# The g2 gain moved into the expert rows on GpSimd, additions to x on VectorE, and two raw weight units turned into units for parts

## The chip, the core and the metric

One core of a Trainium2 chip runs the kernel alone. Its engines are TensorE (PE in the profile; PEld is its weight load), VectorE (DVE), ScalarE (ACT), GpSimd (POOL) and SyncE (SP), which issues the DMA transfers of the weights. The metric is the time of one execution on the device in microseconds; a row of the profile gives times from the start of the span.

## The reference, cut to what matters

A conformer-like block (convolution, attention, memory attention, feed-forward) is followed by a second block: four attention mixers, and then a mixture of 16 experts, of which each of the 256 tokens takes two. The change lies in the experts:

```
score = sigmoid(t @ router_w) + router_bias ...      # two experts per token
for e in range(16):
    he = silu(t @ w_gate[e]) * (t @ w_up[e])         # 2048 -> 512
    y = y + combine[:, e:e + 1] * (he @ w_down[e])   # 512 -> 2048
x = x + g2[:, None] * y
return rmsnorm_2(x, final_g)
```

t is 256 x 2048, all in fp32. Each expert has three matrices of 2048 x 512 numbers, 12 MB together, so the experts read 192 loads of 1 MB. g2 is one row of 2048 gains.

## The kernel before

**Tokens and experts.** x, the 256 tokens, lies in two units of 128 x 2048. Each expert gets at most 64 tokens; these are gathered by products with 0/1 matrices (`gather`, L1917), as a high and a low part in fp32r side by side in one 128-column operand. Two experts share a block of 128 slots. After the down projection `give` (L2074, L2075) writes the 64 rows of an expert into half of the pair's unit `E[e]["out"]`: ScalarE copies the low half from PSUM, VectorE adds the high half.

**Scatter.** When the odd expert of a pair has ended, the pair's 128 rows go back to the tokens: for each of the 2 token tiles and 4 column blocks of 512, a product of the combine weights and the rows (`mm`, L2138) into a PSUM bank, on VectorE a product of the bank with g2 into a small tile (`mul`, L2144), and on GpSimd the addition to x (`add`, L2148). `scatter` lists these steps; `pipeline` puts them into the queue "out". The last pair (experts 14 and 15) goes another way, `last`, which the diff doesn't touch.

**Order of the work.** The weights are a list of loads, each with two chunks. `run` works through the chunks in order: before the products of a chunk it issues the splits of later chunks, as far as lookahead and units allow, and after each chunk `step` takes one entry from each background queue. All engines take their instructions in the order in which they were issued so. A split is a copy to fp32r on ScalarE (`wh`, L146) and the rest on VectorE (`wl`, L147), both into one unit for parts; TensorE multiplies by both (L1933, L1934). One chunk of every six isn't split: it stays in its raw unit and is multiplied in fp32 (L1931).

**Units.** There are 19 units of 128 x 2048 numbers. Some of them form the ring: a weight load takes a unit of the ring, and the unit returns to it when the last chunk of the load has been split, or, for an unsplit chunk, multiplied. The others serve parts, rows, x and constants. `resize(n)` moves n units from the free ones to the ring (n < 0: back, as they come free). The ring has 7 units when the experts are set up; `resize(1)` makes that 8, and `resize(-1)` at the down projection of expert 6 makes it 7. At that of expert 8 one unit is taken for the final gain. The rule for the lookahead, with AHEAD = 4, is

```
if c[3] is not None and not c[7] and self.ahead > self.AHEAD - (len(self.free_units) < 3):
    break
```

so that with fewer than three free units one chunk less is split ahead.

Of the kernel before, what the change touches and what calls it, by code (L numbers as in the profile page):

```python
# [45 lines left out]
class Kernel:  # L46
# [1743 lines left out]
    def after_mix(self):  # L1790

        nc, i = self.nc, self.i
# [11 lines left out]
        t = self.small([128, 256], "ln")  # L1804
# [7 lines left out]
        for tt in range(2):  # L1812
            e = slice(tt * 16, tt * 16 + 16)
# [60 lines left out]
        self.most = self.ctile([128, 1], "mosti", mybir.dt.int32)  # L1874
        nc.vector.tensor_copy(self.most, most)
        self.g2 = self.row(self.mod[5:6, :])
        self.resize(1)

    def logits(self, kt):

# [55 lines left out]
    def experts(self):  # L1936
        nc, i = self.nc, self.i
        E = {}

        def after(q, n, f):  # L1940
            for _ in range(n):
                self.bg(q, lambda: None)
            self.bg(q, f)
# [29 lines left out]
        def whole():  # L1973

            return len(self.loads) % 3 == 0

        def spread(n):

            s, ps = slice(n * 512, n * 512 + 512), self.bank()
            nc.tensor.matmul(ps, self.ones[0:1, :], self.fg[0:1, s], start=True, stop=True)  # L1980
            nc.scalar.copy(self.fg[:, s], ps)
            self.done(ps)
# [60 lines left out]
        def down(e):  # L2043
            src = i["exp_w_down_2"][0, e].rearrange("(j p) n -> p j n", p=128)

            def begin():
                st = E[e]
                self.flush("gu", ("hid", e))
                st["o"] = {}
                if e == 15:  # L2050
                    self.AHEAD = 2
                if e == 6:
                    self.resize(-1)
                if e == 8:
                    self.fg = self.U()
                    nc.gpsimd.dma_start(self.fg[0:1, :], i["final_g_2"].rearrange("(a n) -> a n", a=1))
                    for n in range(4):
                        after("fg", 2 if n else 24, lambda n=n: spread(n))
                if e % 2 == 0:
                    st["out"] = self.U()  # L2060

            def mm(j, b, wh, wl, n):
                st = E[e]
                if j == 0:
                    st["o"][b] = self.bank()
                self.both(st["o"][b], st["hl"][:, j * 128:j * 128 + 128], wh, wl, n, j == 0, j == 3)
                if j == 3 and e < 15:
                    self.bg("give", lambda: give(b))

            def give(b):  # L2070

                o = E[e]["o"][b]
                t = E[e - e % 2]["out"][e % 2 * 64:e % 2 * 64 + 64, b * 512:b * 512 + 512]
                nc.scalar.copy(t, o[64:128, :])  # L2074
                nc.vector.tensor_add(t, o[0:64, :], t)  # L2075
                self.done(o)

            def rows(j, c, wh, wl):
                if j == 0 and c == 0:
                    begin()  # L2080
                for n in range(2):
                    mm(j, c * 2 + n, wh, wl, slice(n * 512, n * 512 + 512))
                if j == 3 and c == 1 and e % 2 == 1:
                    after("out", 3, lambda: None)
                    self.pipeline("out", [scatter(e - 1, tt, b) for tt in range(2) for b in range(4)], 1, e < 13)

            def columns(b, c, wh, wl):
                if b == 0 and c == 0:
                    begin()
                for n in range(2):  # L2090
                    mm(c * 2 + n, b, wh, wl, slice(n * 512, n * 512 + 512))
                if c == 1:
                    for f in last(b):
                        self.bg(f"end{b}", f)

            def last(b):

                s = slice(b * 512, b * 512 + 512)
                x = [self.x[tt][:, s] for tt in range(2)]
                ps, t = [None] * 2, [None] * 2  # L2100

                def sums():
                    for tt in range(2):
                        ts = slice(tt * 128, tt * 128 + 128)
                        ps[tt] = self.bank()
                        nc.tensor.matmul(ps[tt], E[e - 1]["ct"][:, ts], E[e - 1]["out"][:, s], start=True, stop=True)
                    for tt in range(2):
                        t[tt] = self.small([128, 512], "ev")
                        nc.vector.tensor_mul(t[tt], ps[tt], self.g2[:, s])
                    self.done(*ps)  # L2110
                    if b == 3:
                        self.free(E[e - 1]["out"])

                def adds():
                    for tt in range(2):
                        (nc.vector if b == 3 or tt else nc.gpsimd).tensor_add(x[tt], x[tt], t[tt])

                def squares():
                    for tt in range(2):
                        j = self.small([128, 512], "pts", 4)  # L2120
                        nc.scalar.activation(j, x[tt], AF.Square, accum_out=self.s2[:, tt * 4 + b:tt * 4 + b + 1])
                return lambda: give(b), lambda: None, sums, adds, squares


            for n in range(4):
                self.add_load(src[:, n:n + 1, :] if e < 15 else src[:, :, n * 512:n * 512 + 512], 2048)
                for c in range(2):
                    self.add_chunk(c * 1024, 1024,
                                   lambda wh, wl, n=n, c=c: (rows if e < 15 else columns)(n, c, wh, wl), c == 1 and whole())

        def scatter(e, tt, b):
            s = slice(b * 512, b * 512 + 512)
            x = self.x[tt][:, s]
            st = {}

            def mm():
                ps = st["ps"] = self.bank()
                nc.tensor.matmul(ps, E[e]["ct"][:, tt * 128:tt * 128 + 128], E[e]["out"][:, s], start=True, stop=True)  # L2138
                if tt == 1 and b == 3:
                    self.free(E[e]["out"])  # L2140

            def mul():
                st["t"] = self.small([128, 512], "ev")
                nc.vector.tensor_mul(st["t"], st["ps"], self.g2[:, s])  # L2144
                self.done(st["ps"])

            def add():
                nc.gpsimd.tensor_add(x, x, st["t"])  # L2148
            return [mm, mul, add]

        def new_block():
            self.XG = self.big.tile([128, 2, 16, 128], F32R, name=self.name("xg"), tag="big")
# [217 lines left out]
```

## Time and profile before

| what | value |
|---|---|
| runs | 2842.44 us median of 3 (2838.5 to 2842.62) |
| profiled execution | 2838.56 us, span 2836.8 us |
| granted TensorE clock, mean | 0.986 |
| busy share of the span | PE 97%, PEld 85%, DVE 74%, ACT 50%, POOL 11% |
| bytes read | 680.66 MB, 241 GB/s over the span |

The span runs from the first to the last instruction. A busy share is a mean over stages with different limits. Matmuls are pipelined and their ends are modelled, so a busy TensorE isn't TensorE at its peak. Durations of GpSimd are rough. An idle stretch of an engine is put down to what ended it. The experts are the last 600 us or so of the span.

### The profile page before, as it was taken

The numbers are of one execution on the slowest core, as the hardware profiler recorded it, in microseconds if no ns is written. First come the engines' busy times: TensorE is split into PE (matmuls) and PEld (weight loads), VectorE is DVE, ScalarE is ACT, GpSimd is POOL, SyncE is SP. The second block draws the span as 40 slices with busy tenths as digits, with TensorE's granted clock in tenths as the row PEclk, the third lists the DMA queues.
The fourth block names the chain that finished last, engine by engine and source line by source line (L and its number), as shares of the span: only waits on it lengthen the run. The fifth ranks groups of instructions, "written<-read, shape, count | busy, mean of one in ns | idle before, by whom it ended". The sixth has DMA issues, their size and how long they took to land. (4 is left out here: it accounts for less than half of the span.)

```text
span 2836.8 us, 43879 instructions
## 1 busy us (share of the span) xinstructions
PE 2737.7 (97%) x17766; PEld 2399.5 (85%) x17766; DVE 2104.4 (74%) x2679; ACT 1416.6 (50%) x2100; POOL 316.0 (11%) x286
## 2 busy tenths in 40 slices
PE   8999999999999999999999998999999899999997
PEld 8898999998998999897989897988886676666664
DVE  5566658899767668877777776656555689998998
ACT  5534444334444545444444454445554476666665
POOL 0000100000100000001000102111001202222223
PEclk9999999999999999999999999999999899999999
DMA  7577654566667765676667673746565599989895
GB/s 256 191 273 257 223 212 159 178 232 216 248 228 268 258 231 219 241 263 216 252 219 262 214 239 122 288 129 216 171 213 180 202 371 343 338 324 343 321 343 210
DMA packets 201427, 685.77 MB, mean 242 GB/s; under 512 B 12148, under 2 KB 15332, under 8 KB 180356
## 3 DMA queue, kind: packets, MB, share of 16 engines
q1 hardware_dynamic: 194336, 662.94, 64.7%
q0 software_dynamic: 5680, 19.53, 2.6%
q8 instruction: 141, 2.31, 0.3%
q10 hardware_dynamic: 1203, 0.45, 0.1%
q14 instruction: 67, 0.54, 0.1%
HBM read 680.66 MB, written 2.20 MB: 241 GB/s over the span
## 5 line engine op out<-in xcount | busy, mean ns | idle before, releaser
L147 DVE TENSOR_TENSOR u<-u,u 128x1024 fp32r<-128x1024 f32 (+3 forms) x1064 | 1255.1, 1214 | 365.9 <-ACT u L146 363.6
L146 ACT CAST u<-u 128x1024 fp32r<-128x1024 f32 (+3 forms) x1064 | 1014.4, 996 | 640.0 <-DMA u<-in_w_in_dram 170.6
L181 PE MATMUL ps<-u,u 128*128 128x256 f32 (+1 forms) x2184 | 625.5, 286 | 2.6 <-ACT u L146 1.7
L183 PE MATMUL ps<-u,u 128*128 128x256 f32 (+1 forms) x2184 | 621.4, 285 | 2.5 <-DVE u L147 2.5
L182 PE MATMUL ps<-u,u 128*128 128x256 f32 (+1 forms) x2184 | 621.2, 284 | 0.5
L181 PE MATMUL ps<-big,u 128*128 128x256 f32 (+1 forms) x1672 | 478.7, 286 | 2.0 <-DVE u L451 0.8
L183 PE MATMUL ps<-big,u 128*128 128x256 f32 (+1 forms) x1672 | 475.0, 284 | 4.3 <-DVE u L147 4.3
L182 PE MATMUL ps<-big,u 128*128 128x256 f32 (+1 forms) x1672 | 474.8, 284 | 0.1
L181 PEld LDWEIGHTS ps<-u,u 128*128 128x128 f32 (+1 forms) x2184 | 421.1, 193 | 9.9 <-ACT u L146 3.8
L183 PEld LDWEIGHTS ps<-u,u 128*128 128x128 f32 (+1 forms) x2184 | 420.9, 193 | 4.5 <-DVE u L147 4.3
L182 PEld LDWEIGHTS ps<-u,u 128*128 128x128 f32 (+1 forms) x2184 | 421.2, 193 | 1.7 <-DVE u L1309 1.3
L181 PEld LDWEIGHTS ps<-big,u 128*128 128x128 f32 (+1 forms) x1672 | 321.3, 192 | 11.0 <-issue 4.6
L183 PEld LDWEIGHTS ps<-big,u 128*128 128x128 f32 (+1 forms) x1672 | 321.3, 192 | 5.9 <-DVE u L147 5.7
L182 PEld LDWEIGHTS ps<-big,u 128*128 128x128 f32 (+1 forms) x1672 | 321.4, 192 | 1.1 <-DVE big L1309 0.6
L171 PE MATMUL ps<-u,u 128*128 128x512 f32 x736 | 292.0, 397 | 5.4 <-ACT u L146 5.3
L172 PE MATMUL ps<-u,u 128*128 128x512 f32 x736 | 289.4, 393 | 8.0 <-DVE u L147 7.6
L173 PE MATMUL ps<-u,u 128*128 128x512 f32 x736 | 288.1, 391 | 0.0
L1171 DVE SCALAR_TENSOR_TENSOR u<-u,cols,u 128x2048 f32<-128x2048 f32 x96 | 226.3, 2357 | 5.6 <-DMA u<-in_ada_w_dram 5.6
L1933 PE MATMUL ps<-u,xg 128*128 128x512 f32 x416 | 187.8, 451 | 0.4 <-DVE xg L1924 0.3
L172 PEld LDWEIGHTS ps<-u,u 128*128 128x128 f32 x736 | 139.0, 189 | 39.8 <-DVE u L147 12.5
L171 PEld LDWEIGHTS ps<-u,u 128*128 128x128 f32 x736 | 138.9, 189 | 39.6 <-ACT u L146 8.7
L1934 PE MATMUL ps<-u,xg 128*128 128x512 f32 x416 | 167.6, 403 | 0.8 <-DVE u L147 0.7
(374 smaller groups left out, 3077.9 us busy)
## 6 DMA issues: line engine op xcount, KB each, us to landing
u<-in_w_in_dram SPq DMA_DIRECT2D x128, 1024.0 KB, 5.1
u<-in_ada_w_dram SPq DMA_DIRECT2D x96, 1024.0 KB, 5.3
u<-in_w_up_dram SPq DMA_DIRECT2D x88, 1024.0 KB, 5.5
u<-in_exp_w_gate_dram SPq DMA_DIRECT2D x64, 1024.0 KB, 9.6
u<-in_exp_w_up_dram SPq DMA_DIRECT2D x64, 1024.0 KB, 7.3
u<-in_exp_w_down_dram SPq DMA_DIRECT2D x64, 1024.0 KB, 8.2
u<-in_w_down_dram SPq DMA_DIRECT2D x44, 1024.0 KB, 6.6
u<-in_w_o_dram SPq DMA_DIRECT2D x16, 1024.0 KB, 7.1
```

Of the source, the lines that this page charges most:

```text
L146: self.nc.scalar.copy(wh[:, :width], wt)
L147: self.nc.vector.tensor_sub(wl[:, :width], wt, wh[:, :width].bitcast(F32))
L171: nc.tensor.matmul(o, xh[:, ts], wh[:, cs], start=first, stop=False)
L172: nc.tensor.matmul(o, xh[:, ts], wl[:, cs], start=False, stop=False)
L173: nc.tensor.matmul(o, xl[:, ts], wh[:, cs], start=False, stop=last)
L181: nc.tensor.matmul(o, wh[:, cs], xh, start=first and m % 2 == 0, stop=False, **kw)
L182: nc.tensor.matmul(o, wh[:, cs], xl, start=False, stop=False, **kw)
L183: nc.tensor.matmul(o, wl[:, cs], xh, start=False, stop=last, **kw)
L1171: nc.vector.scalar_tensor_tensor(a, wt, self.col["c"][:, kt:kt + 1], a, op0=OP.mult, op1=OP.add)
L1933: self.nc.tensor.matmul(ps, x, wh[:, s], start=start, stop=False)
L1934: self.nc.tensor.matmul(ps, x, wl[:, s], start=False, stop=stop)
```

## The change

The gain g2 is no longer multiplied into each scattered product. GpSimd multiplies it into the pair's 128 rows, in place, one column block at a time, once for both token tiles (`scale`); after two empty steps TensorE scatters the rows, and one step later VectorE adds the bank to x. The pieces go by column block first, then token tile. An empty item between two pieces takes the place of the empty step that `pipeline` put after each step; for expert 13 there is neither, before and after.

The ring gives two of its 7 units to the free ones instead of taking one, the step at expert 6 goes, and AHEAD is 5 instead of 4 from the set-up of the experts on (2 from expert 15, as before).

```
         self.g2 = self.row(self.mod[5:6, :])
-        self.resize(1)
+        self.resize(-2)
+        self.AHEAD = 5
...
                 if e == 15:
                     self.AHEAD = 2
-                if e == 6:
-                    self.resize(-1)
...
-                    self.pipeline("out", [scatter(e - 1, tt, b) for tt in range(2) for b in range(4)], 1, e < 13)
+                    self.pipeline("out", [it for b in range(4) for tt in range(2)
+                                          for it in ([scatter(e - 1, tt, b), []] if e < 13 else [scatter(e - 1, tt, b)])], 1)
...
+            def scale():
+
+                o = E[e]["out"][:, s]
+                if tt == 0:
+                    nc.gpsimd.tensor_mul(o, o, self.g2[:, s])
...
-            def mul():
-                st["t"] = self.small([128, 512], "ev")
-                nc.vector.tensor_mul(st["t"], st["ps"], self.g2[:, s])
+            def add():
+                nc.vector.tensor_add(x, x, st["ps"])
                 self.done(st["ps"])
-
-            def add():
-                nc.gpsimd.tensor_add(x, x, st["t"])
-            return [mm, mul, add]
+            return [scale, lambda: None, lambda: None, mm, add]
```

## Rows read from the trace of the kernel before

**Rows 1.** The page's engine table: busy us (share of the span) xinstructions.

```profile
PE 2737.7 (97%) x17766; PEld 2399.5 (85%) x17766; DVE 2104.4 (74%) x2679; ACT 1416.6 (50%) x2100; POOL 316.0 (11%) x286
```

**Rows 2.** Busy us by stretch, seven bursts; last three columns: clock, DMA share, GB/s.

```profile
2404.00:2432.00 28.00, 25.98 (x113) 18.09 (x112) 27.23 (x26) 14.21 (x19) 15.58 (x8) 0.94 0.96 366
2478.00:2510.00 32.00, 29.78 (x134) 21.41 (x134) 30.48 (x31) 15.56 (x21) 20.74 (x12) 0.95 0.88 324
...
sum 191.00, PE 175.35 PEld 123.64 DVE 186.62 ACT 98.05 POOL 118.74; mean PE 25.05 PEld 17.66 DVE 26.66 ACT 14.01 POOL 16.96
```

**Rows 3.** The same view, the six stretches between the bursts.

```profile
sum 274.00, PE 273.83 PEld 189.66 DVE 239.00 ACT 217.00 POOL 18.18; mean PE 45.64 PEld 31.61 DVE 39.83 ACT 36.17 POOL 3.03
```

**Rows 4.** Timeline of a burst: start, us, engine, line, [idle before, released by].

```profile
2493.42 3.42 DVE L147 TENSOR_TENSOR u<-u,u 128x1024 fp32r<-128x1024 f32 x2
2496.76 0.68 DVE L2144 TENSOR_TENSOR ev<-ps,u 128x512 f32<-128x512 f32 x1
...
2493.57 2.18 POOL L2148 TENSOR_TENSOR u<-u,ev 128x512 f32<-128x512 f32 x1 [1.76 <-DVE ev L2144]
...
2497.59 0.47 PE L1933 MATMUL ps<-u,pts 128*128 128x512 f32 x1 [2.02 <-DVE ev L2144]
```

**Rows 5.** Instructions of one line: count, ns min/median/max, first and last start.

```profile
L147 DVE TENSOR_TENSOR u<-u,u x265: 1206/1216/2316, 2298.8 to 2779.5; 128x1024 fp32r<-128x1024 f32 x133
...
L2148 POOL TENSOR_TENSOR u<-u,ev x50: 1259/2190/2266, 2332.5 to 2777.9; 128x512 f32<-128x512 f32 x50
...
L2075 DVE TENSOR_TENSOR u<-ps,u x52: 674/683/685, 2320.6 to 2771.9; 64x512 f32<-64x512 f32 x52
...
L2281 POOL TENSOR_TENSOR u<-u,u x1: 1736/1736/1736, 2827.6 to 2827.6; 128x512 f32<-128x512 f32 x1
```

**Rows 6.** The same view, weight loads issued by SyncE, 2300 to 2780 us.

```profile
L128 SPq DMA_DIRECT2D u<-in_exp_w_down_dram x53: 327/341/2986, 2301.2 to 2775.4; - x53
L128 SPq DMA_DIRECT2D u<-in_exp_w_gate_dram x52: 367/378/528, 2304.6 to 2757.3; - x52
L128 SPq DMA_DIRECT2D u<-in_exp_w_up_dram x52: 367/368/2301, 2312.5 to 2764.8; - x52
```

**Rows 7.** Who waited for whom, 2300 to 2780: us in total, times, longest.

```profile
SPq L128 <- DVE u L147: 307.6, 86, 8.3
...
PEld ps L1934 <- DVE u L147: 17.5, 49, 0.6
...
PE ps L1933 <- DVE ev L2144: 11.5, 6, 2.0
...
ACT u L146 <- PE ps L1934: 55.6, 49, 3.2
...
ACT u L146 <- DMA u<-in_exp_w_down_dram: 2.0, 2, 1.5
```

**Rows 8.** Busy us by stretch, columns as in rows 2.

```profile
2390.00:2400.00 10.00, 10.00 (x40) 6.74 (x39) 9.23 (x14) 7.82 (x11) 0.00 (x0) 1.00 1.05 386
...
2210.00:2220.00 10.00, 3.50 (x17) 3.53 (x17) 7.70 (x26) 1.04 (x1) 4.38 (x4) 0.50 0.29 106
```

**Rows 9.** Two loads: issue and landing (line view), first product (timeline).

```profile
L128 SPq DMA_DIRECT2D u<-in_exp_w_gate_dram x1: 378/378/378, 2380.1 to 2380.1; - x1
...
DMA to landing us min/median/max: 7.5/7.5/7.5
...
2396.31 0.39 PE L1933 MATMUL ps<-u,xg 128*128 128x512 f32 x1
...
L128 SPq DMA_DIRECT2D u<-in_exp_w_gate_dram x1: 499/499/499, 2752.0 to 2752.0; - x1
...
DMA to landing us min/median/max: 10.4/10.4/10.4
...
2767.74 0.39 PE L1933 MATMUL ps<-u,xg 128*128 128x512 f32 x1
```

## Prediction

> **What bounds the kernel now.** I read the page's engine table first [rows 1]: TensorE is busy 97% of the span, every other compute engine well below (VectorE 74%). A busy TensorE need not be a full one, so I cut the expert stage, where all edits lie, into stretches. After each odd expert up to 13 there is a burst in which the rows of a pair of experts are scattered into x: seven bursts in all. In the seven stretches that hold them TensorE is busy 175.35 of 191 us [rows 2]; in the six stretches between them 273.83 of 274 us [rows 3]. So what another engine can still give back in this stage lies nearly all in the bursts: 15.65 us of idle TensorE. Two burst stretches also ran at a mean clock of 0.94 and 0.95 [rows 2], which costs 28 x 0.06 + 32 x 0.05 = 3.3 us more. Together **19.0 us**, 2.7 per burst.
>
> Who holds TensorE up there? VectorE is busy 186.62 of the 191 us of the bursts [rows 2]. The timeline of one burst shows how [rows 4]: while GpSimd adds a 128x512 piece to x (2.18 us), two weight splits (L147) take 3.42 us together, and the scaling product (L2144) of an earlier scatter comes only after them, at 2496.76. TensorE waits 2.02 us for just that, since the bank which it wants next is the one that L2144 reads. The view of one line gives 1206/1216/2316 ns for a split [rows 5]: alone it costs 1.21 us, beside a GpSimd addition up to 1.1 us more. GpSimd's addition itself ranges from 1.26 to 2.27 us, median 2.19 [rows 5]: each lengthens the other.
>
> Behind VectorE stands the weight stream. All 53 + 52 + 52 = 157 loads of the stage's middle are issued from 2301.2 to 2775.4 us [rows 6], one per 474.2/157 = 3.02 us, and SyncE's wait before them is mostly for L147 (307.6 us), for a unit to come free [rows 7]. The loads are a full 1 MB: at 386 GB/s, the rate with the DMA engines fully busy [rows 8], one needs 2.72 us. DMA isn't the bound on average, but has only a tenth to spare, and it lives on the number of raw units ahead. ScalarE's copies already waited for a load, 2.0 us in two pieces [rows 7]: the present ring is just deep enough.
>
> **The change, part by part.** *GpSimd.* Per burst, eight additions L2148 go and four multiplications of the same shape come. No such multiplication is in this stage's trace; the nearest is the one of the last step, 1.74 us [rows 5], inside the additions' range, so I price it as an addition. Each overlaps one split, so VectorE gets back 4 x 1.1 = 4.4 us per burst; the bounds are 0 (a multiplication that blocks twice as long) and 8.8.
>
> *VectorE.* Eight products from PSUM (0.68 us [rows 4]) become eight additions that read one operand from PSUM and write x. The row with that very form, a sum of PSUM and a unit (L2075), takes 0.68 us too [rows 5]. Nothing gained or lost in busy time; bounds are zero both ways, as neither end of the two rows differs. But the read of the bank is queued one chunk after the scatter instead of two (the step spacing of two chunks stays), so one split fewer stands before the bank comes free: 1.2 to 2.3 us earlier.
>
> *TensorE* scatters the same 8 products, three chunks later. They now wait for GpSimd. The scaling of a column block is issued four chunks or more after the rows are complete and three chunks before its product; a chunk is half a load, 1.51 us, so 4.5 us stand against at most 2.27 us. I cost it at nothing; what covers it are those three chunks, and without cover it costs up to 2.27 us for each of 28 blocks. The row unit is freed three chunks later; that falls within the next pair's first chunks, and both row units fit in the count below.
>
> Sum for the bursts: 4.4 us plus an earlier bank against 2.7 us that TensorE loses. I take 16.0 of the 19.0 us; the lower bound is 8, if the unchanged 8 x 0.68 us of evacuations keep half of the lag.
>
> *The units.* There are 19. x takes 2, h2 2, g2 1. Before: a raw ring of 8 (7 from expert 6), so 6 (7) for parts and rows; with fewer than three free, the split stops with 4 chunks ahead. After: a ring of 5 from the start of the experts, 9 left: 6 chunks ahead, and 5 from expert 8, where the final gain takes a unit. So a load may start three raw units later, but two chunks earlier: 3 x 3.02 - 2 x 1.51 = 6.0 us late up to expert 6; then 2 x 3.02 - 2 x 1.51 = 3.0; from expert 8 2 x 3.02 - 1.51 = 4.5.
>
> What does that meet? Two gate loads, each at the tightest place of its pair, one early and one late in the stage [rows 9]. The one issued at 2380.1 lands 7.5 us later, at 2387.6, and TensorE uses it at 2396.31: 8.7 us after landing (the product is found by counting chunks in order). The one of 2752.0 lands at 2762.4 and is used at 2767.74: 5.3 us. ScalarE's copy and VectorE's split need some 2.3 us of that (an estimate: a split's 1.22 and no more than that for the copy). So 8.7 - 6.0 - 2.3 = +0.4 early, 5.3 - 4.5 - 2.3 = -1.5 us late: about even in the first pairs, and the more so in the one or two that are only 3.0 late, but short by one to two in the last three. A shortage counts once per pair, since in a burst the stream gets ahead again. ScalarE and VectorE take their work in order, so a copy that waits for its load holds up the evacuations behind it; these have TensorE's 5 or 6 split chunks as cover. I take **+6 us** for the stage, bounds 0 and 27 (seven pairs with 6.0 us late on a cover of 5.3, and half a load each).
>
> *Five chunks ahead.* ScalarE waits 55.6 us for TensorE to free a unit for parts, and weight loads wait 17.5 us in 49 pieces for L147 [rows 7]. One chunk more lets splits run ahead over the evacuations. Much of that waiting lies under products still running (the stretches between bursts show 0.17 us idle), so of 0 to 17.5 us I take 2.5, near zero.
>
> Start: while the routing is worked out the ring is full and the DMA engines are busy 0.29 of the time [rows 8]; three units fewer in that queue leave five loads, some 15 us of work, in hand, so I cost the start at nothing. Nothing is added to the last expert's path: 0.
>
> Sum: -16.0 + 6.0 - 2.5 = **-12.5 us**. The profiled execution took 2838.56 us; 2838.56 - 12.5 = 2826.1. The median of the runs is 3.9 us above it, 2842.44, and would give 2829.9. I say **2828 us**.
>
> **A rule of the skill.** The row says that a GpSimd operation costs a split 1.1 us, half of its own 2.19 us [rows 5]. The Trainium skill, "SBUF — State Buffer", section "SBUF: two separate sides", says that a VectorE operation with two SBUF inputs and a GpSimd operation that reads SBUF exclude each other for a whole instruction. By that and the profile's own span, four operations fewer would be worth 4 x 2.19 = 8.8 us per burst instead of 4.4; by either, more than TensorE loses there, so the sum stays. The same rule speaks against the change where GpSimd is the one that waits: the fourth rival.
>
> **Rivals.** *The ring gives it back.* For it: 10% spare on DMA, copies that already waited. If every pair is short by half a load (1.4 us) plus the delay of the evacuations behind it (about 1), the ring costs 7 x 2.4 = 17 us against 18.5: about 2841, no change.
>
> *Half a cure.* VectorE stays near full in a burst because the count of its instructions is the same; the bursts give 8, the ring takes 6: about 2840.
>
> *The ring becomes the bound, slower.* Place: the gate and up loads before each burst. If the lookahead buys nothing (splits stall on the late load, so ring 5 means three loads later and no chunks back), loads come 9.1 us late up to expert 6, 6.0 after; against covers of 8.7 and 5.3 less 2.3 us the pairs lose 2.7 and 3.0, and with the evacuations (about 1.5) some 4.2 each, 29 us: -18.5 + 29, about 2852. It decides once a pair loses more than 18.5/7 = 2.6 us.
>
> *TensorE waits for GpSimd.* VectorE is 98% busy in bursts, GpSimd has to get in between. If each of 28 scalings makes the scatter wait 1 us, 28 us are lost: about 2855. Against it: the additions never exceeded 2.27 us with VectorE that full [rows 5].
>
> **How the numbers follow.** Forecast (bursts cured, ring at 10 us or less): 0.58, 2812 to 2836. No change (first two rivals): 0.24. Ring as bound: 0.14. GpSimd wait: 0.04. 0.2% of 2842.44, 5.7 us, is what a measurement here can tell; the forecast's upper edge and the first rival's lower edge both touch 2836.7, so faster 0.60, same 0.23, slower 0.17. Leaving out 0.1 above and 0.1 below: **2811 to 2847**.
>
> **What would show it.** Right: 28 multiplications and no L2148; splits over 2 us halve in number; TensorE's wait for the bank (11.5 us [rows 7]) gone and burst stretches above 97% busy. ScalarE's waits for DMA grow from 2 us to some tens, without TensorE's idle time growing between bursts. Wrong: TensorE idle before products on weights while the load is on its way, above all in the second half of a pair, or a wait of the scatter for the new multiplication.

## The result and the profile after

The changed kernel takes 2869.23 us (median of 6 runs) beside 2841.31 us for the kernel before on the same chip: ratio 1.0097, 95% interval 1.0082 to 1.0112, 27.5 us slower. The forecast was 2828 us, in a range of 2811 to 2847. The profiled execution took 2869.81 us, its span 2868.0 us, 31.2 us above the span before; the mean granted clock fell from 0.986 to 0.981.

The engine table of the page, which answers to [rows 1]:

```profile
PE 2748.4 (96%) x17766; PEld 2408.2 (84%) x17766; DVE 2094.6 (73%) x2679; ACT 1420.8 (50%) x2100; POOL 289.7 (10%) x258
```

VectorE and GpSimd both have less to do than before, and the kernel is slower. The view by line and form, 2300 to 2780 us (count | busy us, mean ns | idle before, released by), shows the splits and GpSimd's two kinds of work, first of the kernel before:

```profile
L147 DVE TENSOR_TENSOR u<-u,u 128x1024 fp32r<-128x1024 f32 x265 | 349.6, 1360 | 21.1 <-ACT u L146 20.4
L2148 POOL TENSOR_TENSOR u<-u,ev 128x512 f32<-128x512 f32 x50 | 104.9, 2107 | 418.1 <-DVE ev L2144 418.1
L2007 POOL TENSOR_SCALAR bias<-cst,pos,comb 128x64 f32<-128x64 f32 x24 | 19.3, 817 | 0.0
```

and of the kernel after:

```profile
L147 DVE TENSOR_TENSOR u<-u,u 128x1024 fp32r<-128x1024 f32 x248 | 304.2, 1254 | 51.6 <-ACT u L146 49.5
L2140 POOL TENSOR_TENSOR u<-u,u 128x512 f32<-128x512 f32 x24 | 55.2, 2311 | 388.8 <-DVE u L2074 388.8
L2008 POOL TENSOR_SCALAR bias<-cst,pos,comb 128x64 f32<-128x64 f32 x24 | 44.1, 1850 | 0.0
```

A split became 106 ns shorter on average: 106 x 265 = 28 us in some six bursts (50 of the 56 additions lie in these 480 us), 4.5 us per burst, as much as the prediction gave VectorE back. But the splits aren't all of VectorE's work. Two other operations became longer (same two views, before and then after):

```profile
L2038 DVE TENSOR_TENSOR pts<-bias,pts 128x256 fp32r<-128x256 f32 x13 | 5.4, 417 | 0.0
L1904 DVE TENSOR_TENSOR o<-pos,cst 128x128 f32<-128x128 f32 x12 | 2.9, 284 | 0.0
```

```profile
L2039 DVE TENSOR_TENSOR pts<-bias,pts 128x256 fp32r<-128x256 f32 x13 | 12.0, 924 | 0.0
L1905 DVE TENSOR_TENSOR o<-pos,cst 128x128 f32<-128x128 f32 x12 | 9.5, 829 | 0.0
```

Such operations stand at the start of a burst, where the multiplications now fall. By the engine tables VectorE's busy time shrank by only 2104.4 - 2094.6 = 9.8 us, 1.4 us per burst. So some of the relief stayed, and still the kernel lost time. The stretches show why. Each burst begins with the gate and up stage of an odd expert. I cut the first 25 us of these seven stages out of each trace, from the first product of the stage (columns as in [rows 2], whose burst stretches begin some ten us later). The kernel before:

```profile
2394.00:2419.00 25.00, 25.00 (x90) 15.74 (x89) 24.42 (x24) 18.03 (x21) 8.77 (x4) 1.00 1.04 401
...
sum 175.00, PE 174.35 PEld 110.33 DVE 170.10 ACT 123.63 POOL 67.97; mean PE 24.91 PEld 15.76 DVE 24.30 ACT 17.66 POOL 9.71
```

The kernel after, same stages:

```profile
2327.00:2352.00 25.00, 19.77 (x61) 11.26 (x60) 22.43 (x23) 16.05 (x20) 16.06 (x8) 0.93 0.85 316
2404.00:2429.00 25.00, 19.68 (x62) 11.55 (x61) 21.99 (x22) 16.45 (x20) 15.31 (x7) 0.93 0.87 313
...
sum 175.00, PE 144.02 PEld 86.24 DVE 163.94 ACT 114.96 POOL 100.97; mean PE 20.57 PEld 12.32 DVE 23.42 ACT 16.42 POOL 14.42
```

Before, TensorE was idle for 175 - 174.35 = 0.65 us of these 175 us; after, for 31.0 us. On top of it the granted clock, 1.00 in all seven before, averages 0.92 after (0.93, 0.93, 0.86, 0.93, 1.00, 0.86, 0.93), which costs some 0.08 x 175 = 14 us (an estimate). So about 45 us are lost in a place that lost nothing. The six stretches that lie between these seven, before and then after:

```profile
sum 295.00, PE 279.83 PEld 205.81 DVE 259.94 ACT 197.44 POOL 67.45; mean PE 46.64 PEld 34.30 DVE 43.32 ACT 32.91 POOL 11.24
```

```profile
sum 318.00, PE 312.13 PEld 229.67 DVE 256.69 ACT 208.53 POOL 7.86; mean PE 52.02 PEld 38.28 DVE 42.78 ACT 34.75 POOL 1.31
```

There the idle time of TensorE fell from 295 - 279.83 = 15.2 us to 318 - 312.13 = 5.9, and the clock, 0.97 in two of the six before, is 1.00 in all of them: some 12 of the 19 us that the prediction counted did come back. GpSimd is busy 14.4 us of each of the seven stretches instead of 9.7, with half the scatter operations: the multiplications run at the front, and the small products for the next pair's combine weights (L2008) followed them. The DMA engines moved 309 to 333 GB/s there; before, 388 to 401 in six of the seven and 346 in one.

The waits after, 2300 to 2780 us (in total, times, longest), which answer to [rows 7]:

```profile
ACT u L146 <- DMA u<-in_exp_w_down_dram: 52.6, 43, 3.9
...
PEld ps L1935 <- DVE u L147: 45.4, 40, 2.7
...
PE ps L1935 <- DVE u L147: 27.3, 24, 2.3
...
ACT u L146 <- DMA u<-in_exp_w_up_dram: 26.9, 21, 4.9
...
ACT u L146 <- DMA u<-in_exp_w_gate_dram: 16.8, 16, 1.7
...
PE ps L1934 <- DVE u L2149: 0.5, 1, 0.5
```

The wait for the bank is gone (11.5 us before, 0.5 now). ScalarE waits 96.3 us for loads instead of 2.0, and TensorE waits 27.3 us for a split. The waits for a split show at the start of one burst. VectorE and GpSimd there (timeline, as in [rows 4]):

```profile
2332.95 0.68 DVE L2074 TENSOR_TENSOR u<-ps,u 64x512 f32<-64x512 f32 x1
2333.67 1.23 DVE L147 TENSOR_TENSOR u<-u,u 128x1024 fp32r<-128x1024 f32 x1
2334.81 1.52 DVE L2039 TENSOR_TENSOR pts<-bias,pts 128x256 fp32r<-128x256 f32 x1
2336.36 0.68 DVE L2074 TENSOR_TENSOR u<-ps,u 64x512 f32<-64x512 f32 x1
2337.07 1.23 DVE L147 TENSOR_TENSOR u<-u,u 128x1024 fp32r<-128x1024 f32 x1
...
2333.72 2.33 POOL L2140 TENSOR_TENSOR u<-u,u 128x512 f32<-128x512 f32 x1 [90.91 <-DVE u L2074]
2337.12 2.32 POOL L2140 TENSOR_TENSOR u<-u,u 128x512 f32<-128x512 f32 x1 [1.07 <-DVE u L2074]
2340.58 2.34 POOL L2140 TENSOR_TENSOR u<-u,u 128x512 f32<-128x512 f32 x1 [1.14 <-DVE u L2074]
```

and TensorE (same view, same kernel):

```profile
2334.95 0.50 PE L1935 MATMUL ps<-u,xg 128*128 128x512 f32 x1 [1.54 <-DVE u L147]
...
2338.35 0.80 PE L1935 MATMUL ps<-u,xg 128*128 128x512 f32 x1 [2.21 <-DVE u L147]
```

The first two multiplications start 0.1 us after the end of a give (L2074: 2332.95 + 0.68 = 2333.63, then 2337.04). In program order each stands steps later, but GpSimd has nothing else to do and goes as soon as its rows are written. Beside the first one a 128x256 subtraction (L2039), 0.42 us without GpSimd (timeline of the run with the multiplications on VectorE and the same ring), takes 1.52 us; the give and the split behind it come that much later, and TensorE, which has no split chunk in hand, waits 2.21 us for that split. Not all of this is GpSimd's doing. In the run with a marker (below, same ring), where GpSimd multiplies only from 2341.91 on, TensorE waits before the same two products:

```profile
2333.01 0.50 PE L1937 MATMUL ps<-u,xg 128*128 128x512 f32 x1 [1.56 <-DVE u L147]
2335.32 0.49 PE L1937 MATMUL ps<-u,xg 128*128 128x512 f32 x1 [1.11 <-DVE u L147]
```

The first wait is there without GpSimd; of the second, 2.21 - 1.11 = 1.1 us are GpSimd's, as much as the subtraction became longer.

### The profile page after: what moved, and what is told of

It is laid out like the page before. It is cut to its first block, busy times and chain, and to the rows that moved or that the text cites. A ratio compares the mean times of both kernels' runs of the same rounds, so it can differ in the third digit from the quotient of the medians.

```text
span 2868.0 us, 43868 instructions
## 1 busy us (share of the span) xinstructions
PE 2748.4 (96%) x17766; PEld 2408.2 (84%) x17766; DVE 2094.6 (73%) x2679; ACT 1420.8 (50%) x2100; POOL 289.7 (10%) x258
## 5 line engine op out<-in xcount | busy, mean ns | idle before, releaser
L147 DVE TENSOR_TENSOR u<-u,u 128x1024 fp32r<-128x1024 f32 (+3 forms) x1064 | 1228.8, 1186 | 394.6 <-ACT u L146 390.5
```

The lines of the kernel that those rows point to most:

```text
L147: self.nc.vector.tensor_sub(wl[:, :width], wt, wh[:, :width].bitcast(F32))
```

## The experiments

Two theories stood at first. **Theory R**: the smaller ring costs all of the loss, and the scatter part is a gain. **Theory S**: GpSimd's multiplications fall on the gives at the burst's start and hold up the splits. Differences in us below are differences of ratios times 2840 us; an interval of 0.0015 either way is 4 us.

**Halves of the change.** The scatter part alone, with the ring of before (8, then 7 raw units) and four chunks ahead:

```diff
-        self.resize(-2)
-        self.AHEAD = 5
+        self.resize(1)
...
+                if e == 6:
+                    self.resize(-1)
```

> The scatter part alone: g2 into the rows on GpSimd and the addition on VectorE as in the changed kernel; ring (8, then 7) and lookahead (4) as before. Theory R (the smaller ring costs all of the loss, and the scatter part is a gain): faster than before, 2822 to 2833 us; ScalarE's waits for loads stay at some 2 to 10 us between 2300 and 2780. Theory S (GpSimd's multiplications fall on the gives at the start of a burst and hold up the splits there): as slow as the changed kernel or half of it, 2855 to 2870 us, with TensorE waiting for L147 some 25 us.

2852.92 us, ratio 1.0047 [1.0029, 1.0064]: 13 us slower, just under the range of theory S. Theory R falls. The units part alone is the kernel before with the two lines of the units and without `resize(-1)`; the ring alone is the same without `AHEAD = 5`:

> The units part alone: ring 5 from the start of the experts and AHEAD 5; scatter as before (product with g2 on VectorE, addition on GpSimd). Theory R: slower than before by at least the whole loss, 2865 to 2885 us, since the old burst still lengthens eight splits instead of four. Theory S: 2836 to 2848 us, no change.

2874.41 us, 1.0134 [1.0117, 1.0151].

> The ring of 5 with AHEAD 4, scatter as before: three, then two raw units fewer, and the units that come free serve only one more split chunk. Theory R: slower than e2 by the chunk that no longer runs ahead (1.5 us earlier issue per load and less cover): 2870 to 2895 us. Theory S: within 5 us of before.

2871.98 us, 1.0113 [1.0091, 1.0135]: 32 us slower, and five ahead gives nothing back (0.0021 between the two, within their intervals). So neither theory holds alone: both halves are losses.

**Without the multiplication.** From the kernel after, and then from the scatter part alone:

```diff
-                if tt == 0:
-                    nc.gpsimd.tensor_mul(o, o, self.g2[:, s])
+                pass
```

> The changed kernel without GpSimd's multiplication by g2 (the gain is left out of the rows); all else as changed. Theory R: the late loads stay, so it gains only the lengthened splits: 28 x 1.1 us at most where TensorE stands right behind them, 2850 to 2868 us. Theory S: the loss goes, 2830 to 2842 us.

2843.5 us, 1.0013 [1.0004, 1.0023].

> The scatter part alone with the ring of before, as in the run of the scatter part alone (2852.9 us), but GpSimd's multiplication by g2 is left out (so the experts' gain is missing from the result; the rest is computed). Theory S (what GpSimd multiplies at a burst's start costs all of that run's 13 us, and the scatter's other steps are a gain): 2820 to 2832 us. Rival (the scatter's new order costs by itself: the additions to x on VectorE, or the products three chunks later): 2845 to 2856 us.

2828.23 us, 0.9955 [0.9939, 0.9971]. These four runs make a square:

| | GpSimd multiplies | multiplication left out | difference |
|---|---|---|---|
| ring 8/7, four ahead | 1.0047 | 0.9955 | 26 us |
| ring 5, five ahead (after) | 1.0097 | 1.0013 | 24 us |
| difference | 14 us | 16 us | |

Within the intervals the two costs add. The 27.5 us are 26 for the multiplications, 14 for the units, and a gain of 13 from the rest of the scatter's new form (the additions taken off GpSimd, which the next runs price at 21 us, less 8). In the 25 us stretches, the scatter part alone and then the same without the multiplication:

```profile
sum 175.00, PE 154.58 PEld 97.73 DVE 169.85 ACT 115.11 POOL 97.59; mean PE 22.08 PEld 13.96 DVE 24.26 ACT 16.44 POOL 13.94
```

```profile
sum 175.00, PE 166.05 PEld 107.39 DVE 163.94 ACT 122.09 POOL 3.56; mean PE 23.72 PEld 15.34 DVE 23.42 ACT 17.44 POOL 0.51
```

11.5 us of idle TensorE come with the multiplications, and a clock of 0.86 to 1.00 (mean 0.93) instead of 1.00 in all seven, an estimated 0.07 x 175 = 12 us: together 24 of the 26.

**What the old additions cost.** The kernel before without its GpSimd additions (that line replaced by `pass`), with its own ring and with a ring of 5:

> The kernel before without GpSimd's additions to x in the scatter (the experts' rows don't reach x; the rest is computed). It prices the 56 additions. By the prediction (each lengthens a split by 1.1 us, and 19 us of TensorE's idle time and clock go with them): 2820 to 2826 us. Rival (they lie beside slack, and TensorE's waits for a bank come of the products' own lag on VectorE): 2832 to 2840 us.

2817.51 us, 0.9925 [0.9899, 0.9951]: 56 additions cost 21 us, 0.38 us each. 28 multiplications cost 26 us, 0.93 us each.

> Ring of 5, four chunks ahead, the scatter of before, without GpSimd's additions to x (left out as in the run beside it). With the additions that ring cost 32 us. If the smaller ring is dear only where GpSimd makes the splits long (a unit is held longer, so its next load starts later): 2826 to 2842 us, that is some 15 us or less above the run beside it. Rival (the ring is too short for the loads by itself): 2850 to 2862 us, some 30 us above it.

2840.34 us, 1.0002 [0.9991, 1.0014]: the ring of 5 still costs 22 us when GpSimd adds nothing, against 32 beside the additions. It is too short without them too.

**Place.** The multiplications of the scatter part alone, written to one small tile, so that each waits for TensorE's products of the block before:

```diff
-                    nc.gpsimd.tensor_mul(o, o, self.g2[:, s])
+                    E[e]["sg"] = self.small([128, 512], "ev")
+                    self.small([128, 512], "ev")
+                    nc.gpsimd.tensor_mul(E[e]["sg"], o, self.g2[:, s])
...
-                nc.tensor.matmul(ps, E[e]["ct"][:, tt * 128:tt * 128 + 128], E[e]["out"][:, s], start=True, stop=True)
+                nc.tensor.matmul(ps, E[e]["ct"][:, tt * 128:tt * 128 + 128], E[e]["sg"], start=True, stop=True)
...
-            return [scale, lambda: None, lambda: None, mm, add]
+            return [lambda: None, lambda: None, scale, mm, add]
```

> The scatter part alone with the ring of before; the four GpSimd multiplications per burst stay, but each writes one small tile, so that the second to fourth wait until TensorE's products of the block before have read it: they are spread over the burst, some four chunks (6 us) apart, instead of following the gives at its start (1, 2 and 3 each within some 3.5 us). Theory S as to the place (25 us are lost because the multiplications fall together at the burst's start, on the gives and on splits that are just in time): 2829 to 2841 us. Rival (a GpSimd multiplication costs VectorE the same wherever it falls in the burst): 2849 to 2857 us, as the run of the scatter part alone.

2841.07 us, 1.0005 [0.9991, 1.0019], at the upper edge of theory S's range. GpSimd's timeline in it:

```profile
2399.49 1.31 POOL L2143 TENSOR_TENSOR ev<-u,u 128x512 f32<-128x512 f32 x1 [45.96 <-DVE u L2075]
2403.08 2.28 POOL L2143 TENSOR_TENSOR ev<-u,u 128x512 f32<-128x512 f32 x1 [2.27 <-DVE u L2075]
2415.21 2.07 POOL L2143 TENSOR_TENSOR ev<-u,u 128x512 f32<-128x512 f32 x1 [9.86 <-PE ps L2147]
2421.42 1.58 POOL L2143 TENSOR_TENSOR ev<-u,u 128x512 f32<-128x512 f32 x1 [4.14 <-issue]
```

The same work on the same engine, of which only the last two of four come later, costs 14 us instead of 26: 0.50 us each. In the 25 us stretches of its trace TensorE is busy 156.46 us, little more than the 154.58 without pacing, but at a mean clock of 0.97 instead of 0.93 (the profiled execution, 2847.24 us, was one of the longer ones). That the place counts, and not only how much longer VectorE's work becomes, is seen in the engine tables of the five kernels:

| GpSimd's work in the scatter | VectorE busy with it, without it | longer by | time lost by it |
|---|---|---|---|
| 56 additions, kernel before | 2104.4, 2063.7 us | 40.7 us | 21 us |
| 28 multiplications, scatter part alone | 2086.3, 2064.5 us | 21.8 us | 26 us |
| 28 multiplications, paced | 2090.2, 2064.5 us | 25.7 us | 14 us |

One operation lengthens VectorE's work by 0.73 us (additions), 0.78 or 0.92. A microsecond of that costs the kernel 0.5 us, 1.2 us and again 0.5 us. Holding the small products for the combine weights back as well (their tile taken from the same small one) changes nothing:

> The paced run with the ring of before (2841.1 us), and in addition GpSimd's four small products for the next pair's combine weights (L2007) write the same small tile, so that they start only when the burst's last product has read it, and not right behind the last multiplication, in the burst. Theory: part of the 13 us that pacing did not give back is theirs, since they now fall into the burst (3.2 us long after the burst before, 7.9 us in the run of the scatter part alone): 2828 to 2837 us. Rival (the 13 us are the four multiplications' own, wherever they fall): 2838 to 2844 us.

2842.39 us, 1.0015 [1.0, 1.003]. So the 14 us aren't theirs, and are put down to the multiplications. In the changed kernel, with its ring of 5, the same pacing gives nothing:

> The kernel after itself (ring of 5, five ahead) with the multiplications spread over the burst through one small tile, as in the paced run with the ring of before. If place and ring are costs of their own that add: 2869 less the 12 us that pacing gave there, 2853 to 2861 us. If pacing gives more where every load is just in time: 2843 to 2852 us. If it gives nothing here (the ring alone holds the stage): 2866 to 2872 us.

2868.72 us, 1.0104 [1.0074, 1.0134]. It may be that there the first two multiplications, which pacing leaves where they were, are enough; why the last two cost nothing in it is not settled.

A first try at place failed by its own construction: GpSimd was to wait until VectorE had come to its step (`vector.memset(mk)`, then a `gpsimd.tensor_mul` on `mk` ahead of the multiplication).

> The kernel after, but each GpSimd multiplication waits until VectorE has come to its step of the scatter (VectorE writes a 128x8 marker there, GpSimd reads it first), so that it no longer starts right behind the give. Theory S as to the place (the multiplication costs because it falls on the gives and splits at the burst's start): 2846 to 2860 us. Rival (a GpSimd operation costs VectorE the same wherever it falls): 2866 to 2876 us; rival of the prediction (TensorE then waits for GpSimd): above 2876 us, with waits of the scatter product for the multiplication.

2896.54 us, 1.0201 [1.0172, 1.0229], and TensorE's waits in it, 2300 to 2780 us, are led by

```profile
PE ps L2148 <- POOL u L2144: 42.1, 6, 7.9
```

In program order the gives and the splits of chunks up to five ahead stand before the marker, and VectorE came to it only behind them (at 2340.69 in the burst above), while the product that needs the multiplication comes three chunks later. So TensorE waited for VectorE's place in its queue, 7.9 us at the longest. The run says nothing of place.

**The other engine.** One word (`gpsimd` to `vector` in the multiplication), with the ring of before:

> The scatter part alone with the ring of before, the four multiplications by g2 per burst on VectorE instead of GpSimd, at the same steps. Per burst 4 x about 0.7 us more for VectorE, no GpSimd operation. Theory S (overlap with GpSimd is the cost): 2825 to 2840 us, and splits over 2 us gone from the bursts. Rival (VectorE is full in a burst, so any work for it costs its whole length, 7 x 2.8 = 20 us, and GpSimd's cost less): 2850 to 2865 us.

2834.89 us, 0.9990 [0.9977, 1.0003]: 16 us better than on GpSimd, 10 us above no multiplication at all. Part of these 10 us is a wait of the scatter's products for the multiplication (2300 to 2780 us):

```profile
PE ps L2145 <- DVE u L2141: 5.4, 7, 0.9
```

In the 25 us stretches TensorE is busy 160.60 us, and 166.05 without the multiplication: the same 5.4 us. With the scatter two chunks apart in the last burst too, and then with each burst's scatter three chunks later (`after("out", 6, ...)` for 3):

> A try for the fastest kernel: the ring of before, multiplications on VectorE, and the scatter's steps two chunks apart after the last odd expert too (there they are one apart, and that burst was 2.6 us longer than the other six). 2830 to 2835 us; if the last burst's length has another cause: 2834 to 2838 us.

2838.73 us, 0.9997 [0.9983, 1.0011]: the padding gains nothing.

> The same, with every burst's scatter starting three chunks later, clear of the gives and of the gather's last steps. As VectorE takes its work in order, these multiplications do move. If VectorE's load at the start of a burst is what costs: 2825 to 2831 us. Rival (the count of VectorE's operations costs, not their place): within 3 us of the run beside it.

2828.7 us, 0.9963 [0.9951, 0.9976]. The same instructions three chunks later are worth 10 us, and this version beats both kernels, by 10 us and by 38. The wait of the products for the multiplication is gone from its trace, so at least that part of the 10 us is a wait and not VectorE's load at the burst's start; no run separates the rest. Its 25 us stretches:

```profile
sum 175.00, PE 166.03 PEld 106.86 DVE 169.81 ACT 125.04 POOL 4.53; mean PE 23.72 PEld 15.27 DVE 24.26 ACT 17.86 POOL 0.65
```

TensorE is busy 166.03 us, as in the run without the multiplication (166.05), and the clock is 1.00 in all seven. VectorE did 28 multiplications more, at 0.68 us each; placed there they cost nothing that this view shows. The one word in the kernel after:

> The kernel after with one word changed: the multiplications by g2 on VectorE instead of GpSimd, at the same steps (ring of 5, five ahead). With the ring of before that word was worth 18 us (2852.9 to 2834.9). If GpSimd's overlap is the cost here too: 2846 to 2853 us. Rival (with every load just in time the stream sets the pace and VectorE's longer queue counts in full): 2858 to 2870 us.

2874.76 us, 1.0125 [1.0106, 1.0144], with the same trap as the marker:

```profile
PE ps L2144 <- DVE u L2140: 24.0, 6, 5.1
```

Where VectorE is not as far ahead as the program has it, its place in the program is a late place. Less these 24 us it would be where the first range of its expectation had it, but that is only argued.

**Ring sizes.**

> The kernel after with 6 raw units instead of 5 (one unit less for parts, still five ahead). If what the ring costs falls off steeply with each unit: 2853 to 2860 us. If each unit costs a like share of the 16 us between the scatter part alone and the kernel after: 2860 to 2866 us. If five chunks ahead, not the ring, is what costs: 2867 to 2872 us.

2849.11 us, 1.0039 [1.0025, 1.0053]: faster than any line of the expectation. The sixth unit, with one unit less for parts, is worth 16 us, and with it the kernel is no slower than the scatter part alone on the ring of before (1.0047). The loss lies between five and six units.

> As the run with the multiplications on VectorE, but with a ring of 7 raw units up to expert 6 and 6 after, and five chunks ahead: the five chunks ahead at the price of one raw unit instead of two or three. If a unit less is hidden while no GpSimd operation holds up the splits: 2820 to 2838 us, below the run with the ring of before. Rival (each raw unit taken costs a third of what three cost, 32 us): 2838 to 2855 us.

2842.14 us, 1.0014 [1.0001, 1.0028], against 0.9990 with the ring of before: 7 us dearer. But this can't be put down to the ring. TensorE's waits in it, 2300 to 2780 us, are led by

```profile
PE ps L2146 <- DVE u L2142: 18.2, 7, 2.8
```

where the run with the ring of before had 5.4: with five chunks ahead more splits stand before the multiplication in VectorE's queue, the trap of the marker again. What the unit itself costs, this run doesn't show.

> The fastest kernel so far (multiplications on VectorE, scatter three chunks later, two chunks apart; 2828.7 us with the ring of before) with a ring of 6 throughout and five chunks ahead. If a ring of 6 is deep enough once a burst no longer holds up VectorE: 2820 to 2827 us, by the 0.7 to 0.9 us that each even gate and up stage gains with more units for parts. Rival (a raw unit less costs more than that): 2830 to 2842 us.

2829.88 us, 0.9961 [0.9947, 0.9975]: the same as with the ring of before (0.9963). Where the burst no longer holds VectorE up, a ring of 6 with five ahead costs and gains nothing that these runs can tell.

## Why the prediction was wrong, step by step

**What bounds the kernel** held as a reading, and misled as a measure. The 15.65 us of idle TensorE and the low clock are where the GpSimd additions were: without them the kernel is 21 us faster, near the 19.0. But I read "VectorE full" as one condition of a whole burst. The first 25 us of the stage in which it lies were full on VectorE (24.3 of 25 us) and on TensorE alike, with no idle time to give back and none to spare. That stretch I never priced, because nothing was lost in it.

**The step that failed** is the first: "Each overlaps one split, so VectorE gets back 4 x 1.1 = 4.4 us per burst", turned into a gain of 16.0 us. The scatter part alone came out as 13 us lost. The 4.4 us met the 4.5 by which the splits became shorter, but as VectorE's gain it was too much, and that the two agree is luck: not every multiplication falls on a split, and one operation lengthens VectorE's work by some 0.75 us, not 1.1. VectorE got back 18.1 us in the scatter part alone, 2.6 per burst, and 1.4 per burst in the kernel after. What decided was the place, which the step left out: the four multiplications follow at once behind the gives, where no split chunk is in hand, and there a microsecond of VectorE's time cost 1.2 us, where one beside the old additions had cost 0.5. I had taken the multiplication's place from the program ("issued four chunks or more after the rows are complete"). On GpSimd, idle here, that order set nothing; the row that showed it was the release of L2148 by L2144 in [rows 4], a GpSimd operation that started as soon as its data was there.

**GpSimd as something to wait for** at nothing: right. No wait of the scatter product for L2140 is among TensorE's waits after. The fourth rival did not happen; the runs where the product did wait (42.1, 24.0, 18.2 and 5.4 us) had put VectorE's place in its queue before it.

**The earlier bank** was right: 11.5 us of that wait became 0.5.

**The ring** was mis-sized: +6 us for it, measured 14 and 16 us in the square for ring and lookahead together, for which I had 6.0 - 2.5 = 3.5. (The upper bound of 27 doesn't come out of the terms given for it: 7 x (6.0 + 2.3 - 5.3) is 21, with half a load each 31.) The lateness itself was nearly right. The load that answers to the first of [rows 9] (second gate load of expert 5; line view, then the timeline of ScalarE and TensorE, after):

```profile
L128 SPq DMA_DIRECT2D u<-in_exp_w_gate_dram x1: 379/379/379, 2396.4 to 2396.4; - x1
...
DMA to landing us min/median/max: 8.3/8.3/8.3
...
2404.88 1.05 ACT L146 CAST u<-u 128x1024 fp32r<-128x1024 f32 x1 [1.61 <-DMA u<-in_exp_w_gate_dram]
...
2406.32 0.39 PE L1934 MATMUL ps<-u,xg 128*128 128x512 f32 x1
```

It lands at 2396.4 + 8.3 = 2404.7 and is used 1.6 us later, where 8.7 us stood before: 7.1 us late, where I had 6.0. What failed is "A shortage counts once per pair, since in a burst the stream gets ahead again". In six of the seven 25 us stretches of the kernel before the DMA engines are fully busy (share 1.02 to 1.04, about 400 GB/s): that is where the stream gets ahead. With five units it doesn't: 309 to 333 GB/s after, and 355 to 376 GB/s in the run with a ring of 5 and no GpSimd addition. The shortage lasts through the stage. The third rival named this place and 29 us for it; the ring with the old scatter cost 32.

**Five chunks ahead**, -2.5 us: nothing, by the two runs that differ in it alone (old scatter, ring of 5). That the splits then stop at the late load and not at the count fits ScalarE's waits for loads in both (some 90 us), but no run shows it apart.

**The rivals.** The loss is larger than any of them, since each let the scatter part gain. It is the third rival's ring, at about half its price, plus a scatter part of the wrong sign. Most signs of being right came true in the slower kernel: 28 multiplications and no L2148, fewer splits over 2 us (29 in the experts before, 7 after), no wait for the bank. They told of the relief, and not of what it was exchanged for.

**Still open**: why the scatter without any GpSimd work (0.9955) stays 8 us behind the old scatter without its additions (0.9925). The traces show where: in the 25 us stretches TensorE is busy 166.05 us in the one and 175.00 in the other, and from 2300 to 2780 us it waits 8.9 us for a split (13 times) in the one and never in the other. The old scatter has its first products at that place, the new one only three chunks later; whether that is the reason, no run shows. Open too is why pacing helps with the old ring and not with the ring of 5.

## What to carry to other kernels

An instruction on an engine with nothing else to do starts when its data is there (here after 0.1 us), not where the program put it; to move it, give it a dependence on the engine it should follow, and see that this engine comes there in time (the marker cost 42 us of waits). Price a microsecond of a shared resource by the stretch in which it will land: VectorE got 2.6 us per burst back and the scatter part still lost 2 per burst, since what remained fell where TensorE had no chunk in hand. And size a ring by the stretch in which the loads must catch up, not by the mean rate: five units against six were 16 us.

## What the runs showed of the hardware

GpSimd can be kept out for long. In the scatter without multiplications (timeline), VectorE ran twelve splits without a gap while a GpSimd operation on 128x64 elements (0.82 us on average in the kernel before) took 14.88 us:

```profile
2296.66 13.69 DVE L147 TENSOR_TENSOR u<-u,u 128x1024 fp32r<-128x1024 f32 x12
2311.69 1.23 DVE L147 TENSOR_TENSOR u<-u,u 128x1024 fp32r<-128x1024 f32 x1 [1.34 <-ACT u L146]
...
2295.93 14.88 POOL L2007 TENSOR_SCALAR bias<-cst,pos,comb 128x64 f32<-128x64 f32 x1 [60.63 <-PE ps L2015]
```

It ended at 2310.81, in VectorE's first pause (2310.35 to 2311.69), and the splits took 13.69/12 = 1.14 us each, undisturbed. The same 14.88 us come again in the next burst, and in the kernel before without its additions. The Trainium skill, "SBUF — State Buffer", section "SBUF: two separate sides", has the two exclude each other for a whole instruction. The row agrees that GpSimd is shut out, and goes further: not for one instruction but for twelve in a row. In the changed kernel the rows of 2333 us above show both sides by their times. The split at 2333.67 started just before the multiplication at 2333.72 and took its usual 1.23 us; the multiplication took 2.33 us, where the paced run shows some 1.3 at the shortest, and ended at 2336.05; the subtraction behind the split ended only after that, at 2336.33.

A pause of TensorE can be paid twice: in the scatter part alone 11.5 us more idle time came with about 12 us of lower clock in the same 175 us. It need not be: with the multiplications on VectorE TensorE was idle for 14.4 of the 175 us, and the clock was 1.00 in six of the seven stretches and 0.93 in one. The plainest case of both is the kernel after with the multiplications on VectorE (stretches as above):

```profile
2398.00:2408.00 10.00, 7.64 (x28) 4.68 (x26) 6.78 (x10) 6.86 (x10) 0.00 (x0) 1.00 0.95 349
2408.00:2418.00 10.00, 4.68 (x8) 2.64 (x9) 9.87 (x12) 5.84 (x7) 0.00 (x0) 0.52 0.86 310
2418.00:2428.00 10.00, 10.00 (x39) 6.62 (x39) 9.18 (x12) 6.50 (x7) 0.00 (x0) 0.97 0.98 345
```

TensorE was busy 7.64 and then 4.68 of 10 us, and in the second stretch the granted clock was 0.52, nearly all of it at the lower of its two levels, 1.2 GHz of 2.4; it did 8 products there, and 39 in the next.
